# The last part of a down projection in Strassen's block products, and a later transpose of the norm's scale

## The chip, the cores and the metric

The kernel runs on one core of one Trainium2 chip. The metric is device time in microseconds (us) of one execution. "Before" is the kernel as it stood, "after" the changed one.

## The reference

A causal trunk of two layers on 512 tokens of width 1024, all in float32. Layer 0 mixes with a gated convolution and a causal pooling, layer 1 with a chunked spatial gate; each is followed by a gated feed-forward network (FFN) of width 2816. A last RMS norm gives the output.

```python
def rms_norm(x, g):
    return x * lax.rsqrt(jnp.mean(x * x, axis=-1, keepdims=True) + EPS) * g

def gated_conv_ffn(x, w_gate, w_up, conv_w, conv_b, w_down):
    g = causal_dwconv3(x @ w_gate, conv_w) + conv_b
    return (jax.nn.silu(g) * (x @ w_up)) @ w_down

h = x
for layer in range(2):
    h = h + mixer[layer](rms_norm(h, norm_mix[layer]))
    h = h + gated_conv_ffn(rms_norm(h, norm_ffn[layer]), ...)
return rms_norm(h, final_norm)
```

## The kernel before

**Precision.** Each float32 operand of a product is split into a high part, rounded to TensorE's fp32r, and a low part, the rest. A product is three matmuls: high by high, high by low, low by high (`mm3`). ScalarE writes the high part, VectorE subtracts for the low one (`parts`, `split`). In `summed` the low part is made by a ScalarE copy with factor -1 and a GpSimd DMA that adds the source, so VectorE does nothing.

**Order.** The code is a program for a scheduler: it orders each engine's instructions by program order among those that it thinks ready, and gives out buffers of a pool by tag. `inorder` pins an instruction's place; `behind` adds an edge. On the chip each engine runs its list strictly in order.

**The FFN.** Width 2816 is 22 tiles of 128. `Ffn.steps` walks them in steps of two tiles (f = 0, 2, 4, ... 20). Step 0 (`direct`) multiplies plainly and, between its matmuls, gets the norm's 1/rms: `rstd_cols` sums the squares by eight small matmuls, and a short chain on VectorE and ScalarE (L249, L241 to L251) gives one column for each token tile (`rc_f0c` in layer 0, `rc_f1c` in layer 1). `rstd_spread` lays these columns out as a row for all partitions by four transposes on TensorE (L217, tile `ssr_f`) and a ScalarE copy (L220, `rstd_f`). The hook in `hidden` places both by (i, j): i counts the eight contraction tiles, j the four output banks (`gu`), three matmuls each. The other steps (`both`) form gate and up in Strassen's block products (Winograd's form, seven products for eight) over two tiles at once, with products collected in PSUM banks a, e and b. They use the norm's input `hg[k]`, eight pairs of tiles. The rows of activations are made at each step's end.

After a step, `half_down` multiplies four finished tiles of activations with half of the columns of the down weights: 4 token tiles x 4 tiles x 3 matmuls of 512 columns, in layer 1 added into y[t] by VectorE (L1104, times a column of `ffn.cols`). `waiting` holds the steps' rows until they are split into `a_hi` and `a_lo` (L261, L263).

**The end of layer 1.** `last_down` multiplies tiles 18 to 21, all at once, token tile by token tile: two pieces of 512 columns for each, the last piece halved. Each piece adds into y (L1104), squares on ScalarE with a row sum (L1149), and multiplies with the final norm's gain on VectorE (L1152). When a row of 1024 is complete, a short chain (L1157, L1162 to L1165, L1170) makes its 1/rms; VectorE scales the first 672 columns (SHARE, L1167), ScalarE the other 352 (L1171), and two DMAs write them out (L1172, L1173). `root` (L1127) is a Sqrt whose result nothing reads.

Of the kernel before, what the change touches and what calls it, by code (L numbers as in the profile page):

```python
# [32 lines left out]
def tile_trunk(ctx: ExitStack, tc: tile.TileContext, x, norm_mix, norm_ffn, final_norm,  # L33
# [520 lines left out]
    class Ffn:  # L554
# [211 lines left out]
        def hidden(self, f, before=lambda i, j: None):  # L766

            if f == 0:
                def first(i, j):
                    before(i, j)  # L770
                    if (i, j) == (3, 0):
                        nc.vector.tensor_copy(self.cols, self.norm.rstd_cols(inorder))
                    elif (i, j) == (4, 1):
                        self.r = self.norm.rstd_spread(inorder)
# [8 lines left out]

            def split_acts():
                for ft, row in rows:
                    self.act(ft, row)

            return split_acts

        def steps(self, half_down, before=lambda i, j: None):  # L790
            waiting = {}
            for f, part, ready in STEPS:
                waiting[f] = self.hidden(f, before)
                if part is not None:
                    half_down(*part)
                for done in ready:
                    waiting[done]()

    def ffn0(norm):
        nonlocal prm1  # L800
        with tc.tile_pool(name="f0", bufs=1) as ap:
# [8 lines left out]
            ffn.steps(half_down)  # L810
# [270 lines left out]
    def ffn1(norm):  # L1081
        with tc.tile_pool(name="f1", bufs=1) as ap:
# [39 lines left out]
            def last_down(a, b):  # L1122
                fin = wp.tile([P, D], F32, tag="raw", bufs=4, name="fin")
                nc.scalar.dma_start(
                    fin, final_norm.rearrange("(o d) -> o d", o=1).to_broadcast([P, D]))
                root = small[:, 2:3]
                nc.scalar.activation(root, eps, AF.Sqrt)  # L1127
                ch = {}
                for ft in range(a, b):
                    ch[ft] = weights(w_ffn_down[1][ft * P : (ft + 1) * P, :]  # L1130
                                     .rearrange("(k p) c -> p k c", p=P), 1, D, f"dn1_{ft}")

                def lhs(ft, piece):
                    ts_ = slice(piece[0] * P, (piece[0] + 1) * P)
                    return acts[ft][0][:, ts_], acts[ft][1][:, ts_]

                def rhs(ft, piece):
                    c = slice(*piece[1:])
                    return ch[ft][0][:, 0, c], ch[ft][1][:, 0, c]

                yf = {}

                def done(piece, ps):
                    t, c0, c1 = piece
                    dst = y[t][:, c0:c1]
                    add(dst, ps, t)
                    sq = tp.tile([P, S], F32, tag="sq", name=f"sqf{t}_{c0}")[:, : c1 - c0]
                    ss = ssf[:, t, c0 // 256 : c0 // 256 + 1]
                    nc.scalar.activation(sq, dst, AF.Square, accum_out=ss)  # L1149
                    if c0 == 0:  # L1150
                        yf["row"] = ap.tile([P, D], F32, tag="sum", bufs=3, name=f"yf{t}")
                    nc.vector.tensor_tensor(yf["row"][:, c0:c1], dst, fin[:, c0:c1], ALU.mult)  # L1152
                    ms = ssf[:, t, 0:1]
                    if c0 == 0:
                        nc.vector.tensor_scalar(ss, ss, 1.0 / D, EPS, op0=ALU.mult, op1=ALU.add)
                        return
                    nc.vector.scalar_tensor_tensor(ms, ss, 1.0 / D, ms, op0=ALU.mult, op1=ALU.add)  # L1157
                    if c1 < D:
                        return
                    r = tp.tile([P, LINE], F32, tag="rc", name=f"rc_fin{t}")[:, :1]  # L1160
                    sd = work("sd", 1, f"fin{t}")
                    nc.scalar.activation(sd, ms, AF.Sqrt)  # L1162
                    nc.vector.reciprocal(r, sd)
                    nc.vector.scalar_tensor_tensor(ms, ms, r, r, op0=ALU.mult, op1=ALU.mult)
                    nc.vector.tensor_scalar(ms, ms, -0.5, 1.5, op0=ALU.mult, op1=ALU.add)  # L1165
                    lo, hi = slice(0, SHARE), slice(SHARE, D)
                    nc.vector.tensor_scalar(y[t][:, lo], yf["row"][:, lo], r, ms, op0=ALU.mult,  # L1167
                                            op1=ALU.mult)
                    both = ssf[:, t, 1:2]
                    nc.vector.tensor_tensor(both, r, ms, ALU.mult)  # L1170
                    nc.scalar.activation(y[t][:, hi], yf["row"][:, hi], AF.Copy, scale=both)  # L1171
                    nc.sync.dma_start(out[t * P : (t + 1) * P, lo], y[t][:, lo])  # L1172
                    nc.scalar.dma_start(out[t * P : (t + 1) * P, hi], y[t][:, hi])  # L1173

                pieces = [(t, c, c + 512) for t in range(NT) for c in (0, 512)]
                pieces[-1:] = [(NT - 1, 512, 768), (NT - 1, 768, D)]
                down(f"dn{a}", list(range(a, b)), pieces, lhs, rhs, done)
# [47 lines left out]
```

## Time and profile before

| | |
|---|---|
| median of 3 runs | 994.0 us (993.97 to 995.07) |
| profiled execution | 993.98 us, span 992.2 us |
| TensorE clock granted | 0.999 on average |
| TensorE busy (PE) | 980.7 us, 99% |
| VectorE (DVE) | 769.4 us, 78% |
| ScalarE (ACT) | 544.6 us, 55% |
| GpSimd (POOL) | 99.1 us, 10% |
| HBM | 98.42 MB read, 2.10 MB written |

A row of a timeline has the start in us from the span's start, the duration in us, engine, line of the kernel, operation, output<-inputs, shapes and count; in brackets is the idle time of that engine ahead of it and what ended it. PEld is TensorE's weight load. A matmul's duration includes its way through the array: the next one starts earlier than it ends, so TensorE's pace is read from starts. A group's row has busy us and mean ns after the bar. A row of a table by stages has the stretch, its length, the busy us (and instructions) of PE, PEld, DVE, ACT and POOL, the granted clock, the DMA share and GB/s.

### The profile page before, as it was taken

To read this page: it belongs to the slowest core of one execution; us is meant where nothing else is said; L and a number is where in the kernel's file an instruction comes from. 1 tells how busy PE (TensorE), PEld (TensorE's weight loads), DVE (VectorE), ACT (ScalarE), POOL (GpSimd) and SP (SyncE) were. 2 spreads that over 40 slices of the span, in tenths; PEclk is the share of its full clock that TensorE was granted. 3 is DMA by queue.
4 is the path that set the end of the run, shared out by engine and by line. 5 is a ranking of instruction groups with operands and counts; after the bars stand their busy time and mean duration, and the time that the engine had idled before them with its cause. 6 is when DMAs were issued, how large, how long until landed. Compare 5 with 4: busy or idle time off the path is not lost.

```text
span 992.2 us, 15316 instructions
## 1 busy us (share of the span) xinstructions
PE 980.7 (99%) x6049; PEld 880.9 (89%) x6049; DVE 769.4 (78%) x1174; ACT 544.6 (55%) x816; POOL 99.1 (10%) x117
## 2 busy tenths in 40 slices
PE   9999999999999999999999999999999999999997
PEld 6788887999999999999888988889999999999986
DVE  5897458998788887886787665589987779777776
ACT  5623346765465654655568734576655456554544
POOL 2142022100000000000300001210000000000000
PEclk9999999999999999999999999999999999999999
DMA  7442225555455454553433513265554555455512
GB/s 246 130 149 85 86 86 127 127 140 158 129 149 133 129 143 129 149 128 114 128 99 84 174 61 103 57 138 129 149 159 132 136 142 145 122 135 137 139 54 85
DMA packets 85251, 125.10 MB, mean 126 GB/s; under 512 B 4180, under 2 KB 56124, under 8 KB 85180
## 3 DMA queue, kind: packets, MB, share of 16 engines
q1 hardware_dynamic: 76204, 98.24, 31.8%
q0 software_dynamic: 7056, 23.60, 13.1%
q10 hardware_dynamic: 1920, 2.30, 0.7%
q8 instruction: 47, 0.77, 0.3%
q14 instruction: 24, 0.20, 0.1%
HBM read 98.42 MB, written 2.10 MB: 101 GB/s over the span
## 4 chain that ended last, share of the span: by engine, by line
PE 92%; DVE 2%; ACT 1%; issue 1%; DMA 0%; POOL 0%; ACTq 0%; DVEq 0%
PE dn L154 4%; PE dn L156 4%; PE dn L155 4%; PE d L155 3%; PE d L154 3%; PE d L156 3%; PE v L154 1%; PE oo L154 1%; PE oo L155 1%; PE v L155 1%; PE v L156 1%; PE oo L156 1%; PE oe L155 1%; PE oe L154 1%; PE oe L156 1%; PE g_2a L543 1%
## 5 line engine op out<-in xcount | busy, mean ns | idle before, releaser
L154 PE MATMUL dn<-whi_dn,a_hi 128*128 128x512 f32 (+1 forms) x180 | 69.3, 385 | 0.0
L155 PE MATMUL dn<-wlo_dn,a_hi 128*128 128x512 f32 (+1 forms) x180 | 69.3, 385 | 0.0
L156 PE MATMUL dn<-whi_dn,a_lo 128*128 128x512 f32 (+1 forms) x180 | 69.2, 384 | 0.0
L577 DVE SCALAR_TENSOR_TENSOR c<-rows,prm,c 128x512 f32<-128x512 f32 x88 | 63.6, 743 | 0.8 <-ACT c L575 0.8
L154 PE MATMUL d<-a_hi,whi_d 128*128 128x512 f32 x144 | 56.1, 390 | 0.0
L155 PE MATMUL d<-a_lo,whi_d 128*128 128x512 f32 x144 | 56.1, 390 | 0.0
L156 PE MATMUL d<-a_hi,wlo_d 128*128 128x512 f32 x144 | 56.0, 389 | 0.0
L141 POOL DMA_DIRECT2D wlo_g<-raw_g x20 | 17.2, 859 | 385.6 <-ACT wlo_g L140 328.1
L150 DVE TENSOR_TENSOR wlo_dn<-raw_dn,whi_dn 128x1024 fp32r<-128x1024 f32 x22 | 26.9, 1224 | 26.2 <-ACT whi_dn L149 26.1
L680 DVE TENSOR_TENSOR wlo_s34u<-s34u,whi_s34u 128x1024 fp32r<-128x1024 f32 x20 | 24.5, 1225 | 26.9 <-ACT whi_s34u L679 26.9
L1104 DVE SCALAR_TENSOR_TENSOR y<-dn,small,y 128x512 f32<-128x512 f32 (+1 forms) x49 | 33.8, 734 | 9.1 <-PE dn L156 9.1
L156 PEld LDWEIGHTS dn<-whi_dn,a_lo 128*128 128x128 f32 x180 | 33.8, 188 | 7.0 <-DVE a_lo L263 0.2
L154 PEld LDWEIGHTS dn<-whi_dn,a_hi 128*128 128x128 f32 x180 | 33.9, 188 | 6.4
L155 PEld LDWEIGHTS dn<-wlo_dn,a_hi 128*128 128x128 f32 x180 | 33.9, 188 | 6.4
L143 ACT ACTIVATE whi_u<-raw_u 128x1024 fp32r<-128x1024 f32 x21 | 22.1, 1054 | 30.7 <-PE d L155 16.5
L150 DVE TENSOR_TENSOR wlo_d<-raw_d,whi_d 128x1024 fp32r<-128x1024 f32 x18 | 22.0, 1223 | 19.9 <-ACT whi_d L149 19.9
L149 ACT ACTIVATE whi_dn<-raw_dn 128x1024 fp32r<-128x1024 f32 x22 | 23.3, 1058 | 25.4 <-issue 12.6
L261 ACT ACTIVATE a_hi<-s 128x512 fp32r<-128x512 f32 x44 | 27.3, 625 | 17.9 <-PE dn L155 12.3
L585 ACT ACTIVATE s<-c,prm 128x512 f32<-128x512 f32 x44 | 31.2, 714 | 9.1 <-DVE c L577 9.0
L199 ACT ACTIVATE hgh<-h,prm 128x512 fp32r<-128x512 f32 x24 | 17.3, 722 | 33.3 <-DVE h L310 33.2
L141 POOL DMA_DIRECT2D wlo_u<-raw_u x21 | 18.1, 861 | 169.4 <-ACT wlo_u L140 122.1
L210 POOL TENSOR_TENSOR ssq_f<-ssq_f,sq_f 128x512 f32<-128x512 f32 x14 | 19.7, 1411 | 144.1 <-ACT sq_f L209 109.2
(1386 smaller groups left out, 3638.5 us busy)
## 6 DMA issues: line engine op xcount, KB each, us to landing
raw_g<-in_w_ffn_gate_dram SPq DMA_DIRECT2D x40, 512.0 KB, 3.8
raw_u<-in_w_ffn_up_dram SPq DMA_DIRECT2D x40, 512.0 KB, 3.8
raw_dn<-in_w_ffn_down_dram SPq DMA_DIRECT2D x22, 512.0 KB, 3.6
wlo_u<-raw_u POOLq DMA_DIRECT2D x21, 512.0 KB, 5.6
wlo_g<-raw_g POOLq DMA_DIRECT2D x20, 512.0 KB, 4.7
raw_d<-in_w_ffn_down_dram SPq DMA_DIRECT2D x18, 512.0 KB, 3.7
raw_oe<-in_w_out_even_dram SPq DMA_DIRECT2D x8, 512.0 KB, 3.6
raw_v<-in_w_in_odd_dram SPq DMA_DIRECT2D x8, 512.0 KB, 4.4
```

Source lines behind the costliest of these rows:

```text
L141: nc.gpsimd.dma_start(lo, raw, accum_op=ALU.add)
L143: behind(nc.scalar.activation(hi, raw, AF.Copy), first)
L149: behind(nc.scalar.activation(hi, raw, AF.Copy), after[1])
L150: behind(nc.vector.tensor_tensor(lo, raw, hi.bitcast(F32), ALU.subtract), after[0])
L154: nc.tensor.matmul(ps, lhs[0], rhs[0], start=start, stop=False)
L155: nc.tensor.matmul(ps, lhs[0], rhs[1], start=False, stop=False)
L156: nc.tensor.matmul(ps, lhs[1], rhs[0], start=False, stop=stop)
L261: nc.scalar.activation(hi, src, AF.Copy, scale=scale)
L577: nc.vector.scalar_tensor_tensor(c, t[:, i : S + i], prm("cf", i * NF + ft), c, op0=ALU.mult, op1=ALU.add)
L585: nc.scalar.activation(s, c, AF.Silu, bias=self.prm("bf", ft))
L680: nc.vector.tensor_tensor(lo, src, hi.bitcast(F32), ALU.subtract)
L1104: nc.vector.scalar_tensor_tensor(dst, ps, ffn.cols[:, t : t + 1], dst, op0=ALU.mult, op1=ALU.add)
```

## The change

- Tiles 18 to 21 of layer 1's down projection become one 2 x 2 block product in Winograd's form: two halves of the tokens by two tiles each for the left operand, two tiles each by two halves of the columns for the right one. Seven products (order 1, 2, 5, 6, 3, 7, 4), for each of two row blocks, of 2 tiles x 3 matmuls of 512 columns; the last of the 14 is halved in columns. Products 1, 6, 7, 4 collect in one PSUM bank per row block, 5 and 3 in a second, 2 in a third, and VectorE adds a bank into y whenever it holds a wanted sum (13 times with 512 columns, twice with 256).
- The weights' combinations are made by VectorE in place or in two buffers `t1`, `t2` of tag "sum"; of the seven weight operands five are split by `parts` and two by `summed`. The activations' combinations `s1`, `s2`, `a12`, `a21` are made by VectorE, and the blocks' high and low parts are written into `hg`. The rows of the last four tiles are no longer split into `a_hi` and `a_lo`.
- `fin`, the gain, moves from tag "raw" to tag "sum"; the rows of the output from "sum" to "raw".
- The products with the gain go to GpSimd for token tiles 0 to 2; tile 3 stays on VectorE. The first three rows are shared 512 to 512 between VectorE and ScalarE, the last 672 to 352.
- `root` is gone.
- In both layers the hook of `rstd_spread` moves from (4, 1) to (6, 0).
- `steps` returns the rows that are not yet split; layer 0 splits them where it did.

```diff
-    STEPS = [(0, None, [0]), (2, (0, 2, 0), [2]), (4, (0, 2, 1), [4])]
+    STEPS = [(0, None, True), (2, (0, 2, 0), True), (4, (0, 2, 1), True)]
     for f in range(6, NF, 4):
-        STEPS += [(f, (f - 4, f, 0), []), (f + 2, (f - 4, f, 1), [f, f + 2])]
+        STEPS += [(f, (f - 4, f, 0), False), (f + 2, (f - 4, f, 1), f + 4 < NF)]
...
-                    elif (i, j) == (4, 1):
+                    elif (i, j) == (6, 0):
                         self.r = self.norm.rstd_spread(inorder)
...
-            ffn.steps(half_down)
+            ffn.split_acts(ffn.steps(half_down))
...
-                root = small[:, 2:3]
-                nc.scalar.activation(root, eps, AF.Sqrt)
...
+            def finish(t, c0, c1, ssums={}):
...
+                    row = wp.tile([P, D], F32, tag="raw", bufs=4, name=f"yf{t}")
...
+                times = nc.vector if t == NT - 1 else nc.gpsimd
+                times.tensor_tensor(row[:, c0:c1], dst, fin[:, c0:c1], ALU.mult)
...
+                share = SHARE if t == NT - 1 else S
...
+            nc.vector.tensor_tensor(t1, b12, b11, ALU.subtract)
+            put(1, parts, b11)
+            put(2, summed, b21)
+            nc.vector.tensor_tensor(t2, b22, t1, ALU.subtract)
+            put(5, parts, t1)
+            put(6, parts, t2)
+            nc.vector.tensor_tensor(b12, b22, b12, ALU.subtract)
+            put(3, summed, b22)
+            put(7, parts, b12)
+            nc.vector.tensor_tensor(b21, b21, t2, ALU.subtract)
+            put(4, parts, b21)
...
+            block(1, 0, a11)
+            block(2, 1, a12)
+            for n in range(2):
+                nc.vector.tensor_tensor(s1[:, n], a21[n], a22[n], ALU.add)
+            block(5, 4, s1)
+            for n in range(2):
+                nc.vector.tensor_tensor(s2[:, n], s1[:, n], a11[n], ALU.subtract)
+            block(6, 5, s2)
+            for n in range(2):
+                nc.vector.tensor_tensor(a12[n], a12[n], s2[:, n], ALU.subtract)
+            block(3, 6, a12)
+            for n in range(2):
+                nc.vector.tensor_tensor(a21[n], a11[n], a21[n], ALU.subtract)
+            block(7, 2, a21)
+            block(4, 3, a22)
...
+            for i in range(2):
+                add(y[i][:, left], product(1, i), i)
+            for i in range(2):
+                add(y[i][:, left], product(2, i), i)
+                finish(i, 0, 512)
+            for i in range(2):
+                add(y[2 + i][:, right], product(5, i), 2 + i)
+            for i in range(2):
+                add(y[i][:, right], product(6, i), i)
+            for i in range(2):
+                add(y[i][:, right], product(3, i), i)
+                finish(i, 512, D)
+            for i in range(2):
+                add(y[2 + i][:, right], product(7, i), 2 + i)
+                finish(2 + i, 512, D)
+            for i, c0, c1 in ((0, 0, 512), (1, 0, 256), (1, 256, 512)):
+                add(y[2 + i][:, c0:c1], product(4, i, c0, c1), 2 + i)
+                finish(2 + i, c0, c1)
```

More of the change, by code (lines that the diff above doesn't have):

```diff
@@ new lines, in ffn1 @@
+            a = NF - 4
+            rows = {ft: row for ft, row in ffn.steps(half_down, before)}
+            raw = {(i, j): fetch(
+                w_ffn_down[1][(a + 2 * i) * P : (a + 2 * i + 2) * P, j * 512 : j * 512 + 512]
+                .rearrange("(k p) c -> p k c", p=P), 2, 512, f"dn{a}_{i}{j}")
+                for i, j in ((0, 0), (0, 1), (1, 1), (1, 0))}
+            fin = ap.tile([P, D], F32, tag="sum", bufs=3, name="fin")
+            nc.scalar.dma_start(
+                fin, final_norm.rearrange("(o d) -> o d", o=1).to_broadcast([P, D]))
```

137 lines of the change are left out of this document (72 added, 65 removed).

## The prediction

> **What bounds the kernel now.** I read the page first, then a table of the last stages, then the rows of each place that the change touches.
>
> ```profile
> span 992.2 us, 15316 instructions
> PE 980.7 (99%) x6049; PEld 880.9 (89%) x6049; DVE 769.4 (78%) x1174; ACT 544.6 (55%) x816; POOL 99.1 (10%) x117
> PE 92%; DVE 2%; ACT 1%; issue 1%; DMA 0%; POOL 0%; ACTq 0%; DVEq 0%
> ```
>
> TensorE is the bound: 92% of the chain that ended last. VectorE at 78% is an average; what matters is whether it has room in the stage that is rebuilt. Profiled execution: 993.98 us, span 992.2, so 1.78 lies around the span; the median of the three timed runs is 994.0, the same.
>
> The last stages, columns PE, PEld, DVE, ACT, POOL busy: the gate and up products of step 20, the down product of tiles 14 to 17 with the start of the last part, the rest of the last part, the tail.
>
> ```profile
> 932.20:952.30 20.10, 20.10 (x169) 20.10 (x169) 10.46 (x15) 9.96 (x15) 0.00 (x0) 1.00 0.39 106
> 952.30:963.50 11.20, 11.20 (x51) 9.26 (x50) 10.80 (x18) 5.49 (x9) 0.00 (x0) 1.00 0.08 32
> 963.50:985.20 21.70, 21.70 (x107) 18.15 (x105) 16.45 (x41) 9.34 (x24) 0.00 (x0) 1.00 0.19 73
> 985.20:992.20 7.00, 0.00 (x0) 0.00 (x0) 2.47 (x10) 1.38 (x5) 0.00 (x0) 0.87 0.20 75
> ```
>
> VectorE has 9.64 us free in the first, 0.40 in the second, 5.25 in the third: 15.3 before TensorE's end. ScalarE and GpSimd have plenty.
>
> **TensorE's saving.** First and last 512-wide matmul of a run of 21, first and last of the 24 of 256 columns:
>
> ```profile
> 977.40 0.39 PE L154 MATMUL dn<-whi_dn,a_hi 128*128 128x512 f32 x1
> 981.94 0.39 PE L156 MATMUL dn<-whi_dn,a_lo 128*128 128x512 f32 x1
> 982.16 0.28 PE L154 MATMUL dn<-whi_dn,a_hi 128*128 128x256 f32 x1
> 984.92 0.28 PE L156 MATMUL dn<-whi_dn,a_lo 128*128 128x256 f32 x1
> ```
>
> 4.54/20 = 0.227 us and 2.76/23 = 0.12 us apiece. Before: 8 pieces x 12 matmuls, the last piece halved, so 84 x 0.227 + 24 x 0.12 = 21.9. After: 7 products x 2 row blocks x 6 matmuls, one of the 14 halved, so 78 x 0.227 + 12 x 0.12 = 19.1. **Saving 2.8 us**, if nothing makes TensorE wait: its end moves from 985.04 to 982.2.
>
> **What VectorE pays for it.** Groups from 945 to the end, by form (busy, mean ns):
>
> ```profile
> L1104 DVE SCALAR_TENSOR_TENSOR y<-dn,small,y 128x512 f32<-128x512 f32 x11 | 8.0, 746 | 3.2 <-PE dn L156 3.2
> L150 DVE TENSOR_TENSOR wlo_dn<-raw_dn,whi_dn 128x1024 fp32r<-128x1024 f32 x4 | 4.9, 1222 | 1.6 <-ACT whi_dn L149 1.6
> L1152 DVE TENSOR_TENSOR yf<-y,fin 128x512 f32<-128x512 f32 x7 | 4.8, 692 | 0.2
> L263 DVE TENSOR_TENSOR a_lo<-s,a_hi 128x512 fp32r<-128x512 f32 x4 | 2.7, 686 | 0.4 <-ACT a_hi L261 0.4
> L1167 DVE TENSOR_SCALAR y<-yf,rc_fin,ssf 128x672 f32<-128x672 f32 x4 | 2.5, 628 | 0.1
> L738 DVE TENSOR_TENSOR kept<-u_20e,kept 128x256 f32<-128x256 f32 x1 | 0.4, 420 | 0.0
> ```
>
> - Weights: four low parts become five low parts and four combinations of 1024 columns: +5 x 1.222 = +6.1.
> - Activations: four splits of 512 become two splits of 512, ten low parts and eight sums of 256: 18 x 0.42 - 2 x 0.686 = +6.2.
> - Additions into y: seven of 512 become thirteen (the two of 256 stay): +6 x 0.746 = +4.5.
> - Products with the final gain: six of the seven of 512 go to GpSimd: -6 x 0.692 = -4.2.
> - The scaling of three rows goes from 672 to 512 columns: -3 x 0.628 x 160/672 = -0.4.
>
> Sum +12.2 by full durations. Back to back, rows start closer than they last:
>
> ```profile
> 956.95 0.42 DVE L757 TENSOR_TENSOR s<-kept,s 128x256 f32<-128x256 f32 x1
> 957.29 0.42 DVE L758 TENSOR_TENSOR s<-u_20a,s 128x256 f32<-128x256 f32 x1
> 957.62 0.68 DVE L263 TENSOR_TENSOR a_lo<-s,a_hi 128x512 fp32r<-128x512 f32 x1
> ```
>
> 0.34 apart instead of 0.42. With 0.08 off each of the 5 + 16 + 6 - 6 added instructions, net, the sum is +10.5. Room is 15.3 - 2.8 = 12.5, so in total it nearly fits, but not in place. Only three weight combinations and block 1 (3 x 1.22 + 2 x 0.42 = 4.5) need nothing from step 20's activations, which are done at 957.6 and later; they can use the first 9.64. The other 6.0 to 7.7 meet 0.40 + 5.25 - 2.8 = 2.85. **Overhang 3.2 to 4.9 us** of VectorE work behind TensorE's end. The tail absorbs part: VectorE is busy 2.47 of 7.00 there, waiting on ScalarE's root and on its own short chain. About half of those 4.5 idle us can take work of other rows, 1 to 2.2. So the last addition comes 1.0 to 3.9 later behind TensorE's end than today's 985.39 does. I take 1.5, near the low end, because this stretch is back to back.
>
> No stall of TensorE inside the part: product p needs its blocks 2.73 us after the one ahead of it, and the blocks' instructions of VectorE stand ahead of the additions in program order. The additions are what arrives late. The second and third product's weights go through a GpSimd DMA:
>
> ```profile
> wlo_u<-raw_u POOLq DMA_DIRECT2D x21, 512.0 KB, 5.6
> 949.37 1.06 ACT L149 ACTIVATE whi_dn<-raw_dn 128x1024 fp32r<-128x1024 f32 x1
> ```
>
> The second weight buffer comes free at 949.4; 1.1 for the negated copy and 5.6 to land give about 956, for a product due at 963.1 + 2.7 = 965.8: nine us of cover. If that cover were gone, product 2 would wait for all that is missing.
>
> **GpSimd's products.** Two collisions and one control: VectorE's instruction with two SBUF inputs (L200), alone and against a GpSimd product, and an addition with one input in PSUM (L310) under such a product.
>
> ```profile
> 612.32 0.75 DVE L200 SCALAR_TENSOR_TENSOR hgl<-h,prm,hgh 128x512 fp32r<-128x512 f32 x1 [0.79 <-ACT hgh L199]
> 612.95 1.29 POOL L210 TENSOR_TENSOR ssq_f<-ssq_f,sq_f 128x512 f32<-128x512 f32 x1 [1.42 <-ACT sq_f L209]
> 613.56 0.69 DVE L310 TENSOR_TENSOR h<-oo,h 128x512 f32<-128x512 f32 x1 [0.48 <-PE oo L156]
> 615.98 1.68 POOL L210 TENSOR_TENSOR ssq_f<-ssq_f,sq_f 128x512 f32<-128x512 f32 x1 [1.73 <-ACT sq_f L209]
> 616.44 1.78 DVE L200 SCALAR_TENSOR_TENSOR hgl<-h,prm,hgh 128x512 fp32r<-128x512 f32 x1
> ```
>
> A product takes 1.29 alone; against each other L200 took 1.78 instead of 0.75 (+1.03) and the product 1.68 (+0.39), while L310 kept 0.69. So a GpSimd product makes a two-SBUF-input instruction of VectorE wait and leaves the additions alone. Six products: 0 to 6 x 1.29 = 7.7 us of waits. Most of VectorE's work while they run is additions from PSUM, so I take 0.8. The Trainium skill has this as a rule (SBUF — State Buffer, Who interferes with whom): a VectorE instruction with two SBUF inputs and a GpSimd one that reads SBUF exclude each other, and the later one blocks fully. The trace agrees (+1.03); by that rule alone the six would cost up to their full length, which is the slower rival below.
>
> **End stage: -2.8 + 1.5 + 0.8 = -0.5 us** (from -2.8 to +3).
>
> **The rstd transposes of layer 0** move from group (4, 1) to (6, 0):
>
> ```profile
> 158.78 0.39 PE L156 MATMUL gu<-hgh,wlo_g 128*128 128x512 f32 x1
> 161.44 0.62 PE L217 MATMUL ssr_f<-ident,rc_f0c 128*128 128x128 f32 x4 [2.27 <-DVE rc_f0c L251]
> 161.14 0.15 DVE L251 SCALAR_TENSOR_TENSOR rc_f0c<-ms_f0c,rc_f0c 128x4 f32<-128x4 f32 x1
> 170.31 1.37 DVE L624 TENSOR_TENSOR rows<-gu,rstd_f 128x512 f32<-128x512 f32 x2 [0.38 <-PE gu L156]
> 175.12 1.22 DVE L680 TENSOR_TENSOR wlo_s12u<-s12u,whi_s12u 128x1024 fp32r<-128x1024 f32 x1
> 176.46 0.40 PE L543 MATMUL u_2e<-t,whi_s12u 128*128 128x256 f32 x2
> ```
>
> TensorE stands from 159.0 to 161.4 for rc_f0c, 2.4 us. Seven groups of three matmuls now come first, 7 x 0.68 = 4.8, so it reaches the transposes at 163.8, after 161.3: the wait goes. Late next is u_2e: it started at 176.46, just after wlo_s12u was done (175.12 + 1.22 = 176.34), and would now want it at 174.1. VectorE's queue up to there holds 0.38 us of idleness that an earlier gu ends, and some more at ScalarE; one ready product of 1.44 (g_2b) may be slid ahead. Gain 0.4 to 2.4; I take 1.6. The later rstd row is wanted by L624 no earlier than 170.31 - 2.4 = 167.9, four us after the transposes.
>
> **Layer 1:**
>
> ```profile
> 652.70 0.62 PE L217 MATMUL ssr_f<-ident,rc_f1c 128*128 128x128 f32 x4 [0.84 <-DVE rc_f1c L251]
> 661.00:667.40 6.40, 6.40 (x48) 6.05 (x46) 6.40 (x10) 5.48 (x7) 0.86 (x1) 1.00 0.57 167
> 666.25 1.22 DVE L680 TENSOR_TENSOR wlo_s12u<-s12u,whi_s12u 128x1024 fp32r<-128x1024 f32 x1
> ```
>
> The wait is 0.84, but VectorE is full up to the low part that u_2e needs (6.40 of 6.40 us), so TensorE would arrive early and wait there: 0 to 0.84, I take 0.4.
>
> **The dummy root is dropped.** It loaded a table at the very start:
>
> ```profile
> 1.47 1.28 ACT L1127 ACT_TABLE_LOAD   x1 [1.47 <-PEq L1211]
> 32.87 0.20 ACT L241 ACTIVATE sd_m0c<-ms_m0c 128x4 f32<-128x4 f32 x1 [0.73 <-DVE ms_m0c L249]
> ```
>
> If the first load still brings the root's table, nothing changes (taken: 0). If not, 1.28 falls before 32.87, less the 0.73 that ScalarE idles there: at most +0.55.
>
> **Sum:** -0.5 - 1.6 - 0.4 = -2.5: 993.98 - 2.5 = **991.5 us**.
>
> **The rivals.** About 0.2%, 2.0 us, is what a measurement here tells from no change: faster is under 992.0, slower over 996.0.
>
> *Everything comes through* (0.13): VectorE's overhang fits in the tail and both waits vanish: -2.8 - 2.4 - 0.84 = -6.0, 988.0. For it: room of 12.5 against 10.5. Against: the room lies too early.
>
> *VectorE swallows the rstd gain* (0.17): the low part for u_2e comes no earlier, only the end stage counts, with 0.4: -0.9, 993.1. For it: 6.40 of 6.40; against it: 0.38 and more of idleness in layer 0.
>
> *GpSimd's products hold VectorE at the very end* (0.20): VectorE is strictly in order, so a short two-input instruction of a row's root chain that waits for a product holds all additions behind it. Half of 7.7 is 3.9; with an overhang of 3.9 the end stage is -2.8 + 3.9 + 3.9 = +5.0, and with -2.0 from the rstd moves +3.0, 997.0. It decides for slower than before once overhang and waits pass 4.8. For it: +1.03 in the collision above; against it: the additions do not collide.
>
> **How the numbers follow.** Forecast 0.50, its own range 990.0 to 993.0; of it 0.37 lies under 992.0. Faster 0.37 + 0.13 = 0.50; same 0.13 + 0.17 = 0.30; slower 0.20. The range 988.5 to 996.0 leaves out about half of the first rival and two thirds of the last.
>
> **What would show it.** Right: no PE idle before the ssr transposes; the last PE row about 5 us earlier (near 980); VectorE without gaps from about 950 to the last addition, which ends 1.5 us or more behind TensorE. Wrong: PE rows of dn waiting on block or weight parts; u_2e starting where it did; root-chain rows of VectorE of 1 us and more beside GpSimd's products; a second table load near 32 us.

## The result, and the profile after

Four runs of the changed kernel gave a median of **999.99 us** (999.52 to 1000.23), beside 994.52 for four of the kernel before (993.97 to 995.07): ratio 1.0055, 95% interval 1.0042 to 1.0067. The change costs 5.5 us. The prediction was 991.5, range 988.5 to 996.0: the sign is wrong and the range missed. The profiled execution took 1000.23 us, 6.25 more than the one before; its span is 6.3 longer.

The page after: span, busy time, the chain that ended last.

```profile
span 998.5 us, 15341 instructions
PE 979.8 (98%) x6031; PEld 880.0 (88%) x6031; DVE 779.3 (78%) x1195; ACT 552.0 (55%) x829; POOL 108.6 (11%) x125
PE 85%; DVE 7%; issue 2%; ACT 1%; DMA 1%; POOL 0%; DVEq 0%; POOLq 0%; ACTq 0%
```

VectorE has 9.9 us more work than before and TensorE only 0.9 less; VectorE's share of the chain has risen from 2% to 7%. The table by stages, in the stretches in which the prediction read the kernel before:

```profile
932.20:952.30 20.10, 19.26 (x155) 18.82 (x154) 12.45 (x17) 8.12 (x14) 0.00 (x0) 1.00 0.49 149
952.30:963.50 11.20, 11.20 (x61) 9.70 (x60) 11.03 (x18) 9.49 (x14) 1.72 (x2) 1.00 0.31 59
963.50:985.20 21.70, 20.64 (x94) 16.86 (x93) 20.16 (x44) 10.28 (x23) 6.41 (x5) 1.00 0.10 19
985.20:998.50 13.30, 1.48 (x9) 0.98 (x7) 7.38 (x27) 4.46 (x12) 1.50 (x1) 0.66 0.42 158
```

VectorE has become the busy engine of the end (11.03 of 11.20, 20.16 of 21.70) but has 7.65 us free in step 20. To see where time was lost, both traces are compared at the same instructions: start of the first matmul of `oo`, of the last into `g_4a`, last matmul of `g_20a<-t,whi_g`, end of the last addition into y, end of span.

| kernel | oo | g_4a | g_20a | last addition | span |
|---|---|---|---|---|---|
| before | 589.7 | 704.7 | 947.6 | 985.87 | 992.2 |
| after | 588.9 | 706.2 | 949.1 | 990.51 | 998.5 |
| difference | -0.8 | +1.5 | +1.5 | +4.6 | +6.3 |

So layer 0 gains 0.8, the start of layer 1's FFN loses 2.3, the stretch from g_20a to the last addition 3.1, and the tail 1.7 (8.0 instead of 6.3).

**Layer 1's start.** TensorE no longer waits for `rc_f1c`, but stands longer for VectorE's low part, and then runs at half clock (last-but-two column of the stage rows):

```profile
667.64 0.38 PE L543 MATMUL u_2e<-t,wlo_s12u 128*128 128x256 f32 x1 [1.83 <-DVE wlo_s12u L680]
651.90 0.69 DVE L699 TENSOR_TENSOR s12g<-raw_g,raw_g 128x512 f32<-128x512 f32 x1 [0.91 <-DMA t<-t]
668.00:670.00 2.00, 2.00 (x14) 2.00 (x13) 1.49 (x3) 2.00 (x4) 0.00 (x0) 0.66 0.80 150
670.00:672.00 2.00, 2.00 (x12) 2.00 (x11) 2.00 (x3) 1.35 (x4) 0.00 (x0) 0.50 0.12 13
```

**Step 20 and the end part.** VectorE stands at t1 (L1176) and t2 (L1179) for weights, with ready work behind; TensorE waits at g_20e, at product 6 and at the second half of the last piece:

```profile
942.63 1.23 DVE L1176 TENSOR_TENSOR dnt<-raw_dn,raw_dn 128x1024 f32<-128x1024 f32 x1 [3.88 <-DMA raw_dn<-in_w_ffn_down_dram]
943.77 2.35 DVE L150 TENSOR_TENSOR wlo_dn<-raw_dn,whi_dn 128x1024 fp32r<-128x1024 f32 x2
948.70 1.23 DVE L1179 TENSOR_TENSOR dnt<-raw_dn,dnt 128x1024 f32<-128x1024 f32 x1 [2.23 <-DMA raw_dn<-in_w_ffn_down_dram]
949.84 0.42 DVE L743 TENSOR_TENSOR rows<-g_20e,rows 128x256 f32<-128x256 f32 x1
950.31 0.39 PE L543 MATMUL g_20e<-hgh,whi_s34g 128*128 128x256 f32 x1 [0.84 <-DVE rows L743]
...
975.02 0.47 PE L1234 MATMUL dn_a<-whi_dnp,hgh 128*128 128x512 f32 x1 [1.06 <-DVE y L1106]
985.24 0.28 PE L1234 MATMUL dn_a<-whi_dnp,hgl 128*128 128x256 f32 x1
986.87 1.50 POOL L1135 TENSOR_TENSOR yf<-y,fin 128x512 f32<-128x512 f32 x1 [2.55 <-DVE y L1106]
987.16 1.23 DVE L1153 TENSOR_TENSOR ssf<-rc_fin,ssf 128x1 f32<-128x1 f32 x1
988.31 0.47 DVE L1106 SCALAR_TENSOR_TENSOR y<-dn_a,small,y 128x256 f32<-128x256 f32 x1
988.84 0.39 PE L1234 MATMUL dn_a<-whi_dnp,hgh 128*128 128x256 f32 x1 [3.31 <-DVE y L1106]
990.03 0.48 DVE L1106 SCALAR_TENSOR_TENSOR y<-dn_a,small,y 128x256 f32<-128x256 f32 x1 [0.79 <-PE dn_a L1234]
```

The halves of the last piece lie in one PSUM bank. The first was multiplied at 985.5; its addition stood in VectorE's queue until 988.31, and the second half's matmuls waited 3.31 us for that addition. The Trainium skill (PSUM — Partial Sum Buffer, PSUM bank collisions raise a hardware error) says that accesses of different engines are to be kept apart by bank, not by address. The row with the wait agrees; what the wait is worth is a question for a run of its own (halves_last). Directly ahead of that addition stands L1153, a product of 1 column that took 1.23 us beside a GpSimd product.

### The profile page after: what moved, and what is told of

It is laid out like the page before. It is cut to its first block, busy times and chain, and to the rows that moved or that the text cites. A ratio compares the mean times of both kernels' runs of the same rounds, so it can differ in the third digit from the quotient of the medians.

```text
span 998.5 us, 15341 instructions
## 1 busy us (share of the span) xinstructions
PE 979.8 (98%) x6031; PEld 880.0 (88%) x6031; DVE 779.3 (78%) x1195; ACT 552.0 (55%) x829; POOL 108.6 (11%) x125
## 4 chain that ended last, share of the span: by engine, by line
PE 85%; DVE 7%; issue 2%; ACT 1%; DMA 1%; POOL 0%; DVEq 0%; POOLq 0%; ACTq 0%
PE d L154 3%; PE d L155 3%; PE d L156 3%; PE dn L155 3%; PE dn L154 3%; PE dn L156 3%; PE v L154 1%; PE v L155 1%; PE v L156 1%; PE oo L156 1%; PE oo L154 1%; PE oe L156 1%; PE oe L155 1%; PE oo L155 1%; PE oe L154 1%
## 5 line engine op out<-in xcount | busy, mean ns | idle before, releaser
L154 PE MATMUL dn<-whi_dn,a_hi 128*128 128x512 f32 x144 | 56.1, 390 | 0.0
L155 PE MATMUL dn<-wlo_dn,a_hi 128*128 128x512 f32 x144 | 56.1, 390 | 0.0
L156 PE MATMUL dn<-whi_dn,a_lo 128*128 128x512 f32 x144 | 56.0, 389 | 0.0
L150 DVE TENSOR_TENSOR wlo_dn<-raw_dn,whi_dn 128x1024 fp32r<-128x1024 f32 x18 | 21.9, 1223 | 22.6 <-ACT whi_dn L149 22.5
L149 ACT ACTIVATE whi_dn<-raw_dn 128x1024 fp32r<-128x1024 f32 x18 | 19.0, 1058 | 25.1 <-issue 12.3
L261 ACT ACTIVATE a_hi<-s 128x512 fp32r<-128x512 f32 x40 | 24.9, 625 | 13.8 <-PE dn L155 10.2
L200 DVE SCALAR_TENSOR_TENSOR hgl<-h,prm,hgh 128x512 fp32r<-128x512 f32 x24 | 22.1, 922 | 12.8 <-ACT hgh L199 12.7
L156 PEld LDWEIGHTS d<-a_hi,wlo_d 128*128 128x128 f32 x144 | 27.0, 188 | 5.7
L156 PEld LDWEIGHTS dn<-whi_dn,a_lo 128*128 128x128 f32 x144 | 27.0, 188 | 5.7
L1106 DVE SCALAR_TENSOR_TENSOR y<-dn,small,y 128x512 f32<-128x512 f32 x40 | 27.7, 747 | 5.6 <-PE dn L156 5.6
```

Source lines behind the costliest of these rows:

```text
L150: behind(nc.vector.tensor_tensor(lo, raw, hi.bitcast(F32), ALU.subtract), after[0])
L154: nc.tensor.matmul(ps, lhs[0], rhs[0], start=start, stop=False)
L155: nc.tensor.matmul(ps, lhs[0], rhs[1], start=False, stop=False)
L156: nc.tensor.matmul(ps, lhs[1], rhs[0], start=False, stop=stop)
L200: nc.vector.scalar_tensor_tensor(hg[k][1], h[k], g, hg[k][0].bitcast(F32), op0=ALU.mult, op1=ALU.subtract)
L261: nc.scalar.activation(hi, src, AF.Copy, scale=scale)
```

## The experiments

Theory after the result: the end is lost to waits that VectorE's in-order queue makes, layer 1 to a later VectorE and the clock. Rival: GpSimd's products lock VectorE. Ratios are to the runs of the kernel before on the same chip, with 95% intervals. The runs lie on five chips, on which the median of the kernel before is between 994.09 and 995.20, so some tenths between medians of different chips prove little.

| run | median us | ratio |
|---|---|---|
| rstd_l0 | 992.86 | 0.9980 (0.9971 to 0.9988) |
| rstd_l1 | 996.33 | 1.0019 (1.0011 to 1.0028) |
| strassen_only | 999.80 | 1.0051 (1.0038 to 1.0063) |
| halves_last | 999.10 | 1.0043 (1.0029 to 1.0057) |
| gap_filled | 1001.22 | 1.0062 (1.0050 to 1.0075) |
| t2_later | 999.53 | 1.0047 (1.0034 to 1.0060) |
| gain_on_vector | 1000.58 | 1.0051 (1.0037 to 1.0064) |
| products_out | 999.00 | 1.0038 (1.0025 to 1.0050) |
| mid_l1 | 992.88 | 0.9984 (0.9975 to 0.9992) |
| gap_filled2 | 1003.42 | 1.0091 (1.0073 to 1.0109) |
| staggered | 998.68 | 1.0036 (1.0023 to 1.0048) |
| best_of_change | 996.37 | 1.0017 (1.0008 to 1.0025) |
| t1_later | 995.46 | 1.0006 (0.9997 to 1.0015) |
| scale_on_act | 997.28 | 1.0025 (1.0015 to 1.0034) |
| t1_act | 996.39 | 1.0016 (1.0007 to 1.0024) |
| root_first | 995.54 | 1.0008 (0.9999 to 1.0017) |
| rstd_l0_again | 992.92 | 0.9986 (0.9977 to 0.9995) |

**The parts by themselves.** rstd_l0 and rstd_l1 are the kernel before with one layer's hook moved; strassen_only is the kernel after with both hooks back.

```diff
-                    elif (i, j) == (4, 1):
+                    elif (i, j) == ((6, 0) if self.layer == 0 else (4, 1)):   # rstd_l0
+                    elif (i, j) == ((4, 1) if self.layer == 0 else (6, 0)):   # rstd_l1
```

> The kernel before with the rstd transposes at (6, 0) in layer 0 alone. Theory (supply): TensorE's wait of 2.3 us ahead of ssr_f goes, a wait of about 1 us at u_2e comes, the clock stays full: 1.0 us faster than before. Rival (the gain stays whole, what is lost is lost elsewhere): 2.3 us faster.

> The kernel before with the rstd transposes at (6, 0) in layer 1 alone. Theory (supply and clock): VectorE's wlo_s12u ends at the same 667.5, TensorE reaches u_2e 1.8 us too early, and after that gap the granted clock is half for about 3.4 us: 1.5 to 2.5 us slower than before. Rival (the half clock belongs to the rest of the change): within 0.4 us of before, full clock.

> The changed kernel with both rstd transposes back at (4, 1): block products, GpSimd products, root gone. Theory: the end part alone costs 4 to 5 us against before, no half clock near 668; 1 us faster than the changed kernel. Rival (the rstd moves cost most of it): within 2 us of before.

| difference to before | oo | g_4a | g_20a | last addition | span |
|---|---|---|---|---|---|
| rstd_l0 | -1.0 | -1.0 | -1.0 | -1.0 | -1.0 |
| rstd_l1 | +1.1 | +3.5 | +3.5 | +3.5 | +3.6 |
| strassen_only | +0.3 | +0.3 | +0.3 | +3.5 | +5.1 |

By the traces layer 0's move gains 1.0, as its theory had it, layer 1's loses 2.4 from oo to g_4a, and the new last part loses 4.8 by itself. In the medians rstd_l0 is 2.1 faster, near its rival's 2.3, but 12 of the 21 runs of the kernel before on that chip (994.9 to 995.5) have a lower mean clock, some 0.997 for 0.999, as the half clock told of below would give it; against the other nine (993.9 to 994.1) rstd_l0 is 1.1 faster. rstd_l1 is 1.4 slower, just short of its theory, with runs from 994.63 to 997.92. strassen_only is 4.8 slower than before, as its theory had it, but only 0.2 faster than the changed kernel, not 1. In rstd_l1, where layer 0 is untouched, the old wait of 2.3 us in layer 0 was followed by half clock in this execution (the +1.1), and so was the new one in layer 1:

```profile
161.00 1.03 PE L217 MATMUL ssr_f<-ident,rc_f0c 128*128 128x128 f32 x4 [2.28 <-DVE rc_f0c L251]
161.00:166.00 5.00, 5.00 (x17) 4.16 (x18) 5.00 (x10) 3.62 (x6) 0.00 (x0) 0.66 0.60 140
669.75 0.58 PE L543 MATMUL u_2e<-t,wlo_s12u 128*128 128x256 f32 x1 [1.99 <-DVE wlo_s12u L680]
```

**The clock behind the wait.** gap_filled and gap_filled2 put 9 and 12 matmuls of the identity ahead of u_2e in layer 1; the first leaves their place to the scheduler, the second fixes it by dependencies.

```diff
+                if layer == 1 and f == 2 and (key, product) == ("u", 5):
+                    fill = aux_bank("fill")
+                    for n_ in range(9):
+                        inorder(nc.tensor.matmul(fill[:, :P], ident, ident, ...))
```

> The changed kernel with nine small matmuls (the identity by itself, into a spare bank) ahead of u_2e in layer 1, so that TensorE works through most of the 1.83 us in which it waits for wlo_s12u. u_2e itself starts no earlier. Theory (the price of layer 1's wait is the clock that is granted after it: 3.41 us at half clock, 1.7 us of work): the granted clock stays 1.00 from 668 to 672, g_2a's last row comes back by 1.4 to 1.7 and the time falls by about 1.7, from 1000.0 to 998.3. Rival (the clock drop has another cause than the idle time, or the wait alone costs): the drop stays and the time is within 0.4 of 1000.0.

> The changed kernel with twelve small matmuls (the identity by itself, into a spare bank) held by dependencies between g_2e and u_2e in layer 1, in the place where TensorE waits 1.8 to 2.1 us for wlo_s12u; in the earlier try they came out 5 us behind that place. Theory (the half clock behind that wait comes from the idle time, in some executions): the granted clock is 1.00 from 668 to 676, u_2e starts where it did, and the time is that of the changed kernel without the drop, 998.3 to 998.9, in all executions. Rival (the drop doesn't hang on the idle time): clock of 0.5 there in some executions and a time of 999.6 to 1000.2.

Both miss their question. In gap_filled the nine came out at 673.37, behind u_2e, where they cost their own 2.17 us; u_2e waited 2.10 and the clock stayed at 1.00 all the same. In gap_filled2 they took 2.84 us and changed the order of the products, and a new wait of 2.21 at 671.27 was followed by the drop:

```profile
671.27 0.59 PE L543 MATMUL g_2a<-t,whi_s12g 128*128 128x256 f32 x2 [2.21 <-ACT rows L738]
670.00:672.00 2.00, 0.73 (x4) 0.73 (x5) 2.00 (x3) 1.49 (x4) 0.00 (x0) 0.88 0.07 19
672.00:676.00 4.00, 4.00 (x25) 4.00 (x24) 1.42 (x2) 1.32 (x2) 0.00 (x0) 0.63 0.40 125
```

What the other traces show is better evidence. Of the eight executions with the wait of 1.8 to 2.1 us at u_2e, four show half clock behind it (after, rstd_l1, gain_on_vector, staggered) and four don't. halves_last has the very wait of after, 1.83, and no drop:

```profile
667.22 0.38 PE L543 MATMUL u_2e<-t,wlo_s12u 128*128 128x256 f32 x1 [1.83 <-DVE wlo_s12u L680]
668.00:670.00 2.00, 2.00 (x19) 2.00 (x18) 1.74 (x3) 2.00 (x4) 0.00 (x0) 1.00 0.55 102
```

Without the drop its loss from oo to g_4a is 0.9, in after it is 2.3: the wait costs 0.9 to 1.2 (halves_last, t2_later, products_out), the drop some 1.3 more, in half of the executions. All nineteen traces together say more: from 40 to 980 us half clock stands in them eight times, each time behind a wait of TensorE of 1.72 to 2.28 us; six more waits of that size have no half clock behind them, and no trace has half clock without such a wait. So the wait goes ahead of it each time and doesn't decide alone. No kernel that takes away the idle time alone was measured, so that the idle time is the cause rests on this pairing.

**Why VectorE is later in layer 1.** It could be that VectorE is merely full. But L699 waits 0.9 to 1.2 us for a GpSimd DMA of `t` in each kernel with the later transposes, and never in the others, with the same VectorE order. The landing times of that DMA (line L656, from issue; before, then after), and the instruction fetch that lies in 645 to 652 in after alone:

```profile
DMA to landing us min/median/max: 3.3/3.3/4.4
```

```profile
DMA to landing us min/median/max: 3.3/3.6/5.5
q8 instruction: 1, 0.02, 0.8%
```

In all nineteen traces, a fetch between 647.5 and 651.5 goes with the wait (the nine with the transposes at (6, 0), and mid_l1 below), one between 652 and 654.5 with none. To test it, mid_l1 has layer 0's move and layer 1's transposes at (5, 0):

```diff
+                    elif (i, j) == ((6, 0) if self.layer == 0 else (5, 0)):
```

> The kernel before with the rstd transposes of layer 0 at (6, 0) and those of layer 1 at (5, 0), three groups behind (4, 1). In the traces with layer 1's transposes at (6, 0) an instruction fetch falls at 648.5 to 651 (at 652.5 to 654 where they stand at (4, 1)), beside the transfers of t, and VectorE's L699 waits 1.0 to 1.1 for one of them. Theory (the fetch is held back as long as TensorE's queue stands at the transposes, and VectorE is full up to wlo_s12u): at (5, 0) L699 doesn't wait, the 0.84 ahead of the transposes goes and comes back at u_2e, so the time is that of the kernel with layer 0's move alone, 992.9 +-0.4. Rival (any later place lets the fetch come early): L699 waits 1.0 and the time is 994.0 or more. Third (layer 1's wait was worth its 0.84): 992.0.

The median is that of rstd_l0, 992.88: layer 1's 0.84 was worth nothing, as the theory has it. But its eleven runs spread from 992.45 to 994.31, those of rstd_l0 only from 992.36 to 992.99, and the profiled one, the slowest, has the fetch at 647.5 and the wait:

```profile
652.12 0.69 DVE L699 TENSOR_TENSOR s12g<-raw_g,raw_g 128x512 f32<-128x512 f32 x1 [1.21 <-DMA t<-t]
```

So the fetch can come early even here: the theory's mechanism for it (TensorE's queue holds it back) failed, the pairing of fetch and wait held again.

**GpSimd's products.** gain_on_vector gives all of them to VectorE; products_out leaves out the products of the first three rows with the gain.

```diff
-                times = nc.vector if t == NT - 1 else nc.gpsimd
+                times = nc.vector                                   # gain_on_vector
+                if t == NT - 1: times.tensor_tensor(...)            # products_out
+                else: row = y[t]
```

> The changed kernel with all of the final norm's products on VectorE, none on GpSimd. Theory (VectorE's own load in the last 25 us sets the end, the products' collisions are small): six products of 0.61 each, 3.7, come back onto VectorE, less the 1.1 that L1153 waited for a GpSimd product and about 1 of idle time there: 1.5 later, 1001.5. Rival (the collisions with GpSimd cost more than the work taken away): 0.5 to 1.5 earlier, 998.5 to 999.5.

> The changed kernel without the final norm's products by the gain for the first three rows (they are left out, so the output differs): what GpSimd's products cost altogether. Theory (they cost the wait of L1153, 1.1, and little more): 998.9. Rival of the prediction (they hold VectorE by half of their length, 3.9): 996.1. Third, that they cost nothing because VectorE has time: 1000.0.

Without GpSimd's products the row product of one column takes 0.15 us in each of its four places, where one took 1.23 in after; the time is 1.0 less, near the theory's 1.1, and its five runs (997.87 to 999.40) all lie under those of after (999.52 to 1000.23). With them on VectorE the median is 0.6 more, neither the theory's 1.5 nor the rival's gain; the runs overlap and the trace is 0.4 shorter from g_20a to the end, so no difference is shown. GpSimd's products cost about what the prediction took, 0.8, and far from 3.9. The Trainium skill's rule (SBUF — State Buffer, Who interferes with whom) holds in the row quoted above (+1.08), but rarely applies: most VectorE work there reads PSUM. A longer instruction is held in staggered: a scaling of 512 columns took 1.24 us there beside a GpSimd product, 0.55 without one.

**The halves and the order of the last products.** halves_last multiplies both halves of the last piece ahead of both additions; staggered also runs products 7, 3, 4 of one row block, then of the other.

```diff
-                add(y[2 + i][:, c0:c1], product(4, i, c0, c1), 2 + i)
+            halves = [(c, c + 256, product(4, 1, c, c + 256)) for c in (0, 256)]   # halves_last
...
+            for i in range(2):                                                     # staggered
+                add(y[2 + i][:, right], product(7, i), 2 + i); finish(2 + i, 512, D)
+                add(y[i][:, right], product(3, i), i); finish(i, 512, D)
+                # then product 4 of row block i, both halves multiplied first
```

> The changed kernel with the matmuls of both halves of the last piece issued ahead of both additions, so that TensorE doesn't wait for an addition between them. Theory (VectorE's queue holds the end, the 3.3 us wait of TensorE only mirrors it): 1.0 to 1.7 us faster than the changed kernel. Rival (TensorE's wait is the price itself): 3.3 us faster.

> The changed kernel with the last products in another order: 7, 3 and 4 of the first row block, then 7, 3 and 4 of the second, and both halves of the last piece multiplied ahead of both additions. Rows 0 and 2 are then complete 4 us ahead of the end, and only row 3 has its root and its scaling in the tail. Theory (the tail is long because two rows are completed at once, the last addition late because the halves share a bank): 1.4 as with the halves alone, and 2.0 of the tail's 2.4 over before: 996.6. Rival (VectorE's backlog sets the end and an order changes nothing): 998.9 or more.

halves_last gains 1.4 from g_20a to the end of span (48.0 after 49.4) and 0.9 in the medians, not 3.3: VectorE's queue was 2.5 us behind in any case, and the second addition only followed the first more closely. Part of the 1.4 is not the halves': its trace has no wait at g_20e, and gap_filled and gap_filled2, whose end part is that of after, take 48.4 and 48.6 where that wait is at most 0.25. So the halves are worth 0.4 to 0.9. The staggered order adds 0.2 (47.8), not 2.0; in the median, 998.68, it lies near its rival's 998.9. Its tail is still 8.5 long, although only row 3 is completed last.

**Step 20's order.** t2_later puts t2 and b12 behind gate's addition L743; t1_later, on the kernel best_of_change below, puts t1 behind the low part of tile 14's weights, which is ready first and whose buffer the weights for t2 wait for.

```diff
-            nc.vector.tensor_tensor(t2, b22, t1, ALU.subtract)
+            behind(nc.vector.tensor_tensor(t2, b22, t1, ALU.subtract), ffn.added["g"])   # t2_later
-            nc.vector.tensor_tensor(t1, b12, b11, ALU.subtract)
+            behind(nc.vector.tensor_tensor(t1, b12, b11, ALU.subtract),              # t1_later
+                   [x for n, x in lows.items() if n.startswith("dn")][-2])
```

> The changed kernel with the weight combinations t2 and b12 put behind gate's addition L743 of step 20 on VectorE, so that g_20e no longer waits for that addition behind t2's DMA. Theory: the wait of 0.84 at g_20e goes and u_20e comes 0.8 earlier; the end moves by 0.4 to 0.8, since VectorE does t2 0.4 later in turn: 999.2 to 999.6. Rival (VectorE's queue behind 950 sets the end whatever TensorE does): g_20e's wait goes and the last addition stays, 1000.0.

> The kernel of best_of_change (996.4) with the weight combination t1 put behind the low part of tile 14's weights on VectorE. In the traces VectorE stands 3.2 to 4.7 us at t1 for its transfer, while that low part, ready at 940.4, waits behind it; the buffer which it frees is the one that the transfer for t2 waits for, so t2 is held 2.2 us in turn, and g_20e behind it. Theory (the room of step 20 that the prediction counted on is lost in this way): t2 runs 2 to 3 earlier, g_20e no longer waits, VectorE reaches product 5's low parts earlier, and the end comes 1 to 2 earlier: 994.4 to 995.4. Rival (what sets the end comes after 975 alone): 996.4.

t2_later takes g_20e's wait away. Its median, 999.53, lies in its theory's range, but the five runs go from 997.60 to 1000.97, and in the profiled one (1000.65) product 6's wait grows from 1.06 to 2.13, the clock drops behind it and the last addition ends 0.4 later than in after: no gain is shown. t1_later does what was wanted:

```profile
937.54 1.23 DVE L152 TENSOR_TENSOR wlo_dn<-raw_dn,whi_dn 128x1024 fp32r<-128x1024 f32 x1 [1.65 <-ACT whi_dn L151]
939.29 1.23 DVE L1180 TENSOR_TENSOR dnt<-raw_dn,raw_dn 128x1024 f32<-128x1024 f32 x1 [0.53 <-DMA raw_dn<-in_w_ffn_down_dram]
942.57 1.23 DVE L1183 TENSOR_TENSOR dnt<-raw_dn,dnt 128x1024 f32<-128x1024 f32 x1 [0.58 <-DMA raw_dn<-in_w_ffn_down_dram]
```

The transfer waits fall from 3.88 and 2.23 to 0.53 and 0.58, TensorE has no wait at g_20e, and the time falls by 0.9 against best_of_change (995.46 after 996.37), a little less than the 1 to 2 expected. The two ran on different chips, but the slowest run of t1_later, 995.68, is faster than the fastest of best_of_change, 996.00.

**All that cost something undone, and the tail.** best_of_change is staggered with layer 1's hook back and the root kept. scale_on_act, on top of it, gives the scaling of rows 0 to 2 wholly to ScalarE; t1_act joins that with t1_later; root_first is t1_later with ScalarE's scalings of rows 1 and 2 behind the last row's root.

```diff
+            nc.scalar.activation(small[:, 2:3], eps, AF.Sqrt)      # best_of_change
+                wide = hi if t == NT - 1 else slice(0, D)          # scale_on_act: ScalarE's columns
+                if t in (1, 2):                                    # root_first
+                    held.append(scale)
+                    return
```

> The staggered kernel with layer 1's transposes back at (4, 1) and the early root kept: all of the change's parts that cost anything undone but Strassen's products. Theory (the end still costs what TensorE's waits and VectorE's load cost, 1 to 2 more than the 2.8 that it saves): 994.0 to 994.8, above the 992.9 of the kernel before with layer 0's move alone. Rival (with the waits gone TensorE's 2.8 come through): 990.5 to 991.5.

> The kernel of best_of_change (996.4) with the scaling of the first three rows wholly on ScalarE (1024 columns there, none on VectorE). Theory (VectorE, busy without a gap over the last 8 us, sets the end): three instructions of 0.55 and a collision of 0.7 leave it, and the end comes 0.5 to 1.2 earlier: 995.2 to 995.9. Rival (ScalarE's longer scalings hold the last row's root): 996.4 to 997.0.

> Both edits at once on the kernel of best_of_change (996.4). Theory (VectorE's queue is what the end costs): the two gains add, 993.3 to 994.8, still no better than the kernel before with layer 0's move alone (992.9). Rival: no more than the better of the two.

> The kernel of t1_later (995.5) with ScalarE's scalings of rows 1 and 2 put behind the last row's root. In the trace of t1_later the last addition ends at 984.99 and the last row's second square waits until 986.24 and its root until 987.88, each right behind an earlier row's scaling of 0.72 that waits for VectorE; alone they would be done near 986.1. Theory (ScalarE's order is what the longer tail costs): the tail falls from 8.4 to about 6.5, the time by 1.5 to 2.1, to 993.4 to 994.0. Rival (VectorE's queue holds the last row's chain anyway): 0.5 or less, 995.0.

> The kernel before with layer 0's rstd transposes at (6, 0) alone, a second time, to compare with root_first on one chip: 992.9 as in its first run. If Strassen's products pay at all once their waits are gone, root_first is under it; theory: root_first stays 0.5 or more above it.

best_of_change misses its theory by 1.6 on the slow side. Its profiled execution is its slowest, 999.10, where the other ten took 996.0 to 996.8: TensorE waited longer at g_20e, and half clock followed:

```profile
948.80 0.39 PE L543 MATMUL g_20e<-hgh,whi_s34g 128*128 128x256 f32 x1 [1.72 <-DVE rows L743]
950.00:952.00 2.00, 2.00 (x12) 2.00 (x11) 2.00 (x4) 0.43 (x1) 0.00 (x0) 0.50 0.02 4
```

scale_on_act and t1_act go the rival's way, and past it (0.9 slower than best_of_change and t1_later): ScalarE seems to be in the tail's chain as well. In t1_later the last row's square and root stand behind scalings of earlier rows that wait for VectorE:

```profile
985.61 0.72 ACT L1157 ACTIVATE y<-yf,ssf 128x512 f32<-128x512 f32 x1 [0.36 <-DVE rc_fin L1149]
986.24 0.40 ACT L1132 ACTIVATE sqf<-y 128x256 f32<-128x256 f32 x1
986.54 0.19 ACT L1132 ACTIVATION_READ_ACCUMULATOR sqf<-y 128x1 f32 x1
987.25 0.72 ACT L1157 ACTIVATE y<-yf,ssf 128x512 f32<-128x512 f32 x1 [0.53 <-DVE ssf L1143]
987.88 0.19 ACT L1148 ACTIVATE sd_fin<-ssf 128x1 f32<-128x1 f32 x1
```

root_first brought that root forward by 1.0, to 986.86, and the time stayed: 995.54, as its rival had it. But the trace shows another queue than the rival's: with three rows written so late, the output's transfers run at a DMA share of 1.0 until 992 (column before last).

```profile
989.00:990.00 1.00, 0.00 (x0) 0.00 (x0) 0.00 (x0) 0.46 (x1) 0.00 (x0) 0.50 1.03 385
990.00:991.00 1.00, 0.00 (x0) 0.00 (x0) 0.00 (x0) 0.00 (x0) 0.00 (x0) 0.50 1.02 395
991.00:992.00 1.00, 0.00 (x0) 0.00 (x0) 0.00 (x0) 0.00 (x0) 0.00 (x0) 0.50 0.98 363
```

On that chip the kernel of rstd_l0 had 992.92 (rstd_l0_again). The best version of the block products that was tried is 2.6 slower than the kernel before with one hook moved, which beats both kernels.

## Why the prediction was wrong, by its own steps

- **TensorE's saving, 2.8.** The counts are right (18 matmuls fewer), the saving was not reached: TensorE's own waits in the last stages are 0.84, 1.06 and 3.31.
- **VectorE's added work, +12.2 by durations, +10.5 back to back.** Measured over the whole run +9.9: right.
- **"They can use the first 9.64" is the step that failed first.** The three combinations and block 1 did run there, but VectorE's free time in step 20 was counted as room without asking when the weights land. VectorE stands 3.88 and 2.23 there, with ready work behind it, which is pushed into the full stretches: the stage holds only 2.0 us more of VectorE's work than before (12.45 after 10.46) where 4.5 were to fit. t1_later gets 0.9 of it back.
- **"No stall of TensorE inside the part" is wrong.** The blocks and weights did come in time, as argued, and product 2's GpSimd DMA kept its cover (issued at 953.40, landed within 5.1 us, wanted at 968.36). But the products share PSUM banks with the additions, so a late addition stops TensorE. Overhang was put behind TensorE's end; it came back as TensorE's waits, and the last addition starts 0.46 behind the last matmul's start, as it did before (0.47). From g_20a to the last addition the part lost 3.1 where the sum had -0.5.
- **The tail was given no term.** It grew from 6.3 to 8.0. All four rows are now scaled in the last 13 us (ScalarE's four scalings start between 986.11 and 994.53), where they came one in each quarter of the part. The load of the root's table on ScalarE, 1.28 us, moved with the first complete row from 970.35 to 982.36; no run moved it by itself. VectorE's chain, ScalarE's order and the output's transfers each stand ready to hold the tail; staggered, scale_on_act and root_first each eased one, and gained 0.2, lost 0.9 and gained nothing.
- **GpSimd's products, 0.8.** About right: 1.0 without them. The rival that came nearest, 997.0, named the mechanism (a short instruction of VectorE held by a product, additions behind it), but it accounts for 1 us, not 3.9. That its end stage, +5.0, comes near the measured +4.8 is luck.
- **Layer 0's rstd, -1.6 taken.** In the trace -1.0: the 2.27 wait goes, and u_2e, which the text named as "late next", waits 0.93 for `wlo_s12u`:

```profile
175.58 0.38 PE L543 MATMUL u_2e<-t,wlo_s12u 128*128 128x256 f32 x1 [0.93 <-DVE wlo_s12u L680]
```

In the medians it is -2.1 and -1.2, since in part of its executions the kernel before seems to pay for half clock behind that wait, as rstd_l1 shows it in layer 0.
- **Layer 1's rstd, -0.4 taken, bounds 0 to 0.84 of gain.** Sign wrong: +0.9 to +1.2, with a late transfer of `t` ahead of VectorE's low part, and +1.3 more when the clock drops. "VectorE is full up to the low part" was seen; a loss was excluded without reason.
- **The root, 0 taken, bound +0.55.** The second table load did come, and TensorE waits for it:

```profile
32.13 1.28 ACT L241 ACT_TABLE_LOAD   x1
34.63 0.50 PE L154 MATMUL ac<-hgh,whi_ac 128*128 128x512 f32 x1 [0.42 <-ACT whi_ac L149]
```

With the root kept (best_of_change) there is no such wait. In strassen_only, whose layer 0 is otherwise that of before, oo comes 0.3 later: within the bound.

Two of the prediction's signs of being wrong came, the second table load and a root-chain row of 1.23 us beside a GpSimd product, and one of its signs of being right: no wait ahead of the ssr transposes.

Taken together: after against before is -1.0 (layer 0), +0.3 (root), +2.3 (layer 1 with the drop), and +4.8 behind g_20a, where the sum had -1.6, 0, -0.4 and -0.5. So the end stage is 5.3 of the error of 8.7, layer 1 2.7. Of the +4.8, the halves are worth 0.4 to 0.9, GpSimd's products about 1.0 and the order in step 20 0.9, each measured by itself; they overlap, since without GpSimd's products the second half's wait is itself shorter:

```profile
986.61 0.39 PE L1237 MATMUL dn_a<-whi_dnp,hgh 128*128 128x256 f32 x1 [2.18 <-DVE y L1106]
```

So about half of the end stage's loss is not traced to one of these. What of it belongs to which of the three queues in the tail isn't settled: each was moved by itself and another took its place.

## What to carry to other kernels

Free time of an engine in an earlier stage is room only for work whose inputs have landed and which nothing blocked stands ahead of: check the transfer, and the buffer that the transfer waits for. Where an accumulation bank is read by the engine that gets more work, its backlog becomes TensorE's wait, so bank reuse belongs into the sum. A change that completes several output rows at once moves scaling and writing into the tail, and a wait of some 2 us that is only moved can return with a lower clock behind it.

## What of the hardware was not expected

- **A wait of 1.7 to 2.3 us sometimes costs twice.** Behind 8 of 14 such waits in nineteen traces the granted clock is 0.5 for 3.4 us (0.66 on average over 161 to 166 in rstd_l1), and 1.3 us are lost. The same wait of 1.83 was followed by the drop in after and not in halves_last. The Trainium skill (TensorE: Matmul & The Clock Gate, What's actually happening) tells of a free-running window of 3.41 us by which the clock is halved; the length of the drop agrees, the chance would follow from where the wait falls in the window, which no run here shows. But the Trainium skill asks there for an idle window of that length, and the waits ahead of these drops were shorter. The runs of the kernel before lie in two groups, 993.8 to 994.4 with a mean clock of 0.998 to 0.999 and 994.8 to 996.1 with 0.996 to 0.997; rstd_l0, without that wait, has only 992.4 to 993.2.
- **An instruction fetch of 0.02 MB goes with a neighbour's transfer that is a microsecond late.** Where it falls among the transfers of `t`, the slowest of them lands after 5.5 instead of 4.4 us. Four transposes moved by a few groups were enough to shift it by 3 to 5 us. That the fetch delays the transfer, and not a third thing both, is not shown.
- **A square root whose result nobody reads was worth about 0.3 us**: it is the first table load of the kernel before (1.47), and without it another line's load comes first and the root's own, 1.28 us, falls at 32.13, with a wait of TensorE of 0.42 behind it.
